# A chunked recurrence's triangular inverse by blocks of 16, and low-rank products in plain fp32 from the rows themselves

## The chip, the cores and the metric

The kernel runs on one core of a Trainium2 chip. Times are device microseconds (us) of that core for one execution, and a kernel's time is the median of its runs. The engines are PE (TensorE: matrix products), DVE (VectorE), ACT (ScalarE), POOL (GpSimd) and SP (which issues transfers). Each works through a queue of its own in order.

## The reference

One inference step of a two-layer encoder in float32, for 1024 new tokens of one stream and 64 of another, with 1024 features. The first layer mixes time with RWKV-7, the second is sliding-window attention; both end in a SwiGLU network. The change lies in the time mixing. `x` is the normalised input, `x_prev` the same rows one token earlier:

```python
xx = x_prev - x
xr, xw, xk, xv, xa, xg = (x + xx * mu[i] for i in range(6))
r, k, v = xr @ w_rkv[0], xk @ w_rkv[1], xv @ w_rkv[2]
w_log = -softplus(-(w0 + tanh(xw @ w1) @ w2)) - 0.5
decay = exp(-exp(w_log))
a = sigmoid(a0 + (xa @ a1) @ a2)
g = sigmoid(xg @ g1) @ g2
...
def step(s, inp):                       # per head, s is 64 x 64
    r_t, w_t, k_t, v_t, a_t, b_t = inp
    sa = einsum('bhvk,bhk->bhv', s, a_t)
    s = s * w_t[:, :, None, :] + sa[..., None] * b_t[:, :, None, :] + v_t[..., None] * k_t[:, :, None, :]
    return s, einsum('bhvk,bhk->bhv', s, r_t)
```

`w1` and `a1` have 64 columns, `g1` has 160 (in the kernel 128, `g1a`, and 32, `g1b`). There are 16 heads of 64.

## The kernel before

Features lie on the partitions, tokens in the columns. The tokens are two halves: A, the first 512, in one group of columns; B, the other 512 and the second stream's 64 (580 columns with those between the streams, in two groups of 290; 576 in two of 288 later). A dense product cuts both operands into two parts of the type float32r, high and low, and adds three products (lines 422 to 424: high by high, low by high, high by low). The parts are made by a copy on ACT and a subtraction on DVE or POOL. The weights stream in from memory and are cut in the same way (lines 382, 383).

The time mixing goes in stages. For each of the six mixed inputs and each of 8 tiles of features, `mix` (from line 663) multiplies the rows on ACT (line 666), adds the preceding rows on DVE (line 667), and cuts the result (lines 414, 415). The mixes for `v`, `r` and `k` feed dense products (`rkv`). Those for `w`, `a` and `g` feed the low-rank products: `low_step` (line 474) adds what a tile of features gives, 2 products for w1, 2 for a1, 3 for g1a and 2 for g1b for each group of columns, and `streamed` hands it the tiles one by one. `decay`, `rate` and `gate` then make the decays, `a` and `g` from the sums. The weights of the low-rank products are cut in `low` (lines 456, 457).

The recurrence takes 64 tokens at a time: 17 chunks, 8 of half A, 8 of half B, and the second stream. For each chunk `prep` makes the triangles of products of keys and queries; `prep2` calls `inverse`; `chain` carries the state through products with the inverse W (line 277 copies what goes into the product with W); `post` normalises the outputs. What doesn't need the state is made a chunk ahead. `inverse` takes (I - T D)^-1 for a strict triangle T of 64 for each of 16 heads. The two diagonal blocks of 32 are solved by substitution on DVE: each partition is a lane that holds a head's block and a fourth of its rows. There are 15 steps of two columns. In each, the rows are in two halves, a multiplication for each half (line 216) and then a reduction for each (line 220), so that no instruction reads what the one right before it has written. Then the block beside the two is made with two rounds of 16 small products (32 by 32) on PE, a copy by ACT and DVE behind each (lines 243 to 255). W is one buffer.

What stands where in the engines' queues is set by a scheduler, from priorities that the code gives: the recurrence stands ahead, and the dense products beside it fill PE's queue. During chunks 0 to 7 those are half B's products for v, r and k, during chunks 8 to 16 the output product of half A's mixing and half A's first SwiGLU network. The queues are fixed when the program is built.

Of the kernel before, what the change touches and what calls it, by code (L numbers as in the profile page):

```python
# [48 lines left out]
class Rwkv:  # L49
    """The chunked WKV-7 recurrence: chunks of 64 tokens, 16 heads in 8 pairs."""  # L50
# [31 lines left out]
    def start(self):  # L82
        """the part of W that stays zero"""
        nc = self.nc
        self.W = self.sb.tile([128, 8, 64], F32, name="W", tag="W", bufs=1)
        nc.gpsimd.memset(self.W, 0.0)

    def prep(self, ch):
        """all that does not need the state; heads 2j on partitions 0-63, heads 2j + 1 on 64-127"""
# [13 lines left out]
        # 1 / |kk|^2 as the lanes of inverse() hold it: [(parity, half of the tokens, 4 times, pair), token]  # L103
# [9 lines left out]
        nl = self.t([128, 32], "nl", 3)  # L113
        V.transpose(out=nl, in_=n4)

        # the products of the decays up to each token, and before it
# [17 lines left out]
        # kk a / P and -kk Pex without the norm of kk, whose square inverse() divides by  # L134
# [3 lines left out]
        # r k r_k  # L138
# [3 lines left out]
        # the four triangles of each head: [(b, k) of the key, (a, r) of the query]  # L142
# [10 lines left out]
        # sum(r k r_k) v  # L153
# [7 lines left out]
    def prep2(self, d):  # L161
# [4 lines left out]
        # the strict triangle of b is spent: a takes its place  # L166
# [13 lines left out]
    def inverse(self, X, nl):  # L180
        """D (I - T D)^-1 of the strict triangles T, transposed, with D = 1 / |kk|^2: first the blocks of 32 by
        substitution, a lane for each block and each fourth of its rows, then the block beside them"""
# [4 lines left out]
        st = self.t([128, 1024], "f4", 2)  # L187
        for q in range(4):
            d = 32 * (q % 2)
            src = Xh[d:d + 32, :, q // 2, d:d + 32].rearrange("p j t -> p t j").unsqueeze(2).broadcast_to([32, 32, 4, 8])  # L190
            S.copy(st[32 * q:32 * q + 32].rearrange("p (t g j) -> p t g j", g=4, j=8), src)  # L191
        N12 = self.t([128, 8, 32], "in12")
        S.copy(N12[0:32], Xh[0:32, :, 0, 32:64])
        S.copy(N12[64:96], Xh[0:32, :, 1, 32:64])
        NL = self.t([128, 1024], "f4", 2)
        V.transpose(out=NL, in_=st)
        NL = NL.rearrange("p (a b) -> p a b", a=32)
        V.tensor_tensor(out=NL, in0=NL, in1=mid(nl, 32), op=ALU.mult)
        # two columns j, j + 1 at a time: row j + 1 takes what it adds by way of column j
        one = NL.rearrange("p a b -> p (a b)")[:, 32:1024:66]  # L200
        ev = NL.rearrange("p (a two) b -> p a two b", two=2)
        # Z: rows 8 r + 4 h + (0 .. 3) in the half h, so that neither half waits for what it has just written
        Z = self.t([128, 1024], "f4", 2).rearrange("p (h c r b) -> p h c r b", h=2, c=4, r=4)
        tm = Z.rearrange("p h c r b -> p (h c r b)")[:, 0:512].rearrange("p (a b) -> p a b", b=32)
        V.tensor_tensor(out=tm, in0=bc(one, 32), in1=ev[:, :, 0, :], op=ALU.mult)
        V.tensor_tensor(out=ev[:, :, 1, :], in0=ev[:, :, 1, :], in1=tm, op=ALU.add)
        for i in (0, 3):
            V.tensor_tensor(out=Z[:, :, i], in0=c["xl0"].rearrange("p (h a b) -> p h a b", h=2, a=4),
                            in1=nl.unsqueeze(1).unsqueeze(1).broadcast_to([128, 2, 4, 32]), op=ALU.mult)
        for j in range(30, 0, -2):  # L210
            # from the first place to the last, and back
            a, b = (0, 3) if j % 4 else (3, 0)
            part = [(h, (j // 4 + 1 - h) // 2) for h in range(2) if (j // 4 + 1 - h) // 2 < 4]
            for h, r0 in part:
                n = 4 - r0
                V.tensor_tensor(out=Z[:, h, 1:3, r0:4, 0:j],  # L216
                                in0=Z[:, h, a, r0:4, j:j + 2].rearrange("p r c -> p c r").unsqueeze(3).broadcast_to([128, 2, n, j]),
                                in1=NL[:, j:j + 2, 0:j].unsqueeze(2).broadcast_to([128, 2, n, j]), op=ALU.mult)
            for h, r0 in part:
                V.tensor_reduce(out=Z[:, h, b, r0:4, 0:j], in_=Z[:, h, min(a, 1):min(a, 1) + 3, r0:4, 0:j].rearrange("p c r j -> p r j c"),  # L220
                                axis=AX.X, op=ALU.add)
        XL = Z[:, :, 0]
        q4 = lambda x: x.rearrange("p h r (q f) -> p h (r q) f", f=4)[:, :, :, 0:2]
        V.tensor_copy(q4(XL), q4(Z[:, :, 3]))
        xe = XL.rearrange("p h r (a two) -> p h r a two", two=2)
        tm = Z[:, :, 1, :, 0:16]
        V.tensor_tensor(out=tm, in0=xe[:, :, :, :, 1], in1=one.unsqueeze(1).unsqueeze(1).broadcast_to([128, 2, 4, 16]), op=ALU.mult)
        V.tensor_tensor(out=xe[:, :, :, :, 0], in0=xe[:, :, :, :, 0], in1=tm, op=ALU.add)
        D3 = self.t([128, 3, 8, 32], "ixd")
        XD, WD, QT = D3[:, 0], D3[:, 1], D3[:, 2]  # L230
        for h in range(2):
            XO = Z[:, h, 1].rearrange("p a b -> p (a b)")                   # [s, (r g pair)]
            V.transpose(out=XO, in_=XL[:, h].rearrange("p a b -> p (a b)"))
        for h in range(2):
            XO = Z[:, h, 1].rearrange("p a b -> p (a b)").rearrange("p (r g j) -> p j r g", r=4, g=4)
            V.tensor_copy(WD.rearrange("p j (r h g) -> p h j r g", r=4, h=2)[:, h], XO)
        V.transpose(out=XD.rearrange("p a b -> p (a b)"), in_=WD.rearrange("p a b -> p (a b)"))
        for q in range(4):
            f = (q % 2) * 32
            e = V.tensor_copy if q % 2 else S.copy  # L240
            e(W[32 * q:32 * q + 32, :, f:f + 32], WD[32 * q:32 * q + 32])
        ps = self.pc()[:, 0:256].rearrange("p (a b) -> p a b", a=8)
        for j in range(8):
            for lo in (0, 64):
                self.mm(ps[lo + 32:lo + 64, j, :], lhsT=N12[lo:lo + 32, j, :], rhs=XD[lo:lo + 32, j, :],
                                 start=True, stop=True)
# [93 lines left out]
class Dense:  # L340
# [124 lines left out]
    def low_step(self, ps, w, k, x, groups):  # L465
# [4 lines left out]
        if k == 7:  # L470
            parts.reverse()
# [90 lines left out]
def tile_stream_step(ctx: ExitStack, tc: tile.TileContext, I, O):  # L562
# [168 lines left out]
    def rate(half, hs, two):  # L731
# [6 lines left out]
        for (o, n), p in zip(groups, ps):  # L738
            dn.stack(y, dn.low_sum(p, 64, n), slice(o, o + n))
# [673 lines left out]
```

## Time and profile before

| | us |
|---|---|
| median of three runs | 3092.23 |
| lowest and highest run | 3085.42, 3095.97 |
| span of the profiled execution | 3098.9 |
| PE busy | 2948.1 |
| DVE busy | 1905.6 |
| ACT busy | 1371.1 |
| POOL busy | 921.6 |
| first PE product of the time mixing starts at | 25.8 |

The profile is one execution; only its span, from the first to the last instruction, is known, and it is longer than the three timed runs. Busy time of PE counts products with modelled ends, so a busy PE may still be slow: the granted clock says how fast it was. Rows of a group read: line, engine, operation, tile written and tiles read, shapes, count, then busy time in us and the mean of one in ns, then the engine's idle time before them and what ended it. Rows of a timeline read: start, length in us, engine, line, operation, tiles, shapes, count.

### The profile page before, as it was taken

How to read it: one execution, taken by the hardware profiler on the slowest of the kernel's cores; microseconds unless marked ns; L12 is line 12 of the kernel's file. 1: busy time of each engine (PE TensorE's matmuls, PEld its weight loads, DVE VectorE, ACT ScalarE, POOL GpSimd, SP SyncE). 2: the span in 40 equal slices, each digit the busy share in tenths (PEclk: the TensorE clock that was granted, in tenths of full speed). 3: DMA queues.
4: the chain of work that ended last, by engine and by line, in shares of the span. 5: the costliest groups of instructions: out<-in, count | busy, mean ns of one | idle time of the engine just before them, and what ended most of it. 6: DMA issues, size and time to landing. Idle time of an engine off the chain costs nothing. (4 is left out here: it accounts for less than half of the span.)

```text
span 3098.9 us, 52449 instructions
## 1 busy us (share of the span) xinstructions
PE 2948.1 (95%) x20126; PEld 2520.6 (81%) x20126; DVE 1905.6 (61%) x3964; ACT 1371.1 (44%) x2489; POOL 921.6 (30%) x768
## 2 busy tenths in 40 slices
PE   6899898998899999999999999999999999999998
PEld 5677677886677777887778999888667889899998
DVE  8887788968898984356654333565555334633334
ACT  6767655434555442344553222344454233322222
POOL 6464233423333322224311222243111222322221
PEclk9998778988899999999999999999999999999999
DMA  4645443334223224332212222222122332322222
GB/s 143 171 121 152 116 123 91 106 99 143 79 83 96 86 66 127 103 112 84 70 45 69 82 82 82 76 84 82 55 65 65 96 96 75 102 83 83 85 85 69
DMA packets 262051, 289.16 MB, mean 93 GB/s; under 512 B 125028, under 2 KB 143972, under 8 KB 261800
## 3 DMA queue, kind: packets, MB, share of 16 engines
q1 hardware_dynamic: 261800, 285.81, 30.8%
q8 instruction: 158, 2.59, 0.3%
q14 instruction: 93, 0.76, 0.1%
HBM read 243.18 MB, written 41.16 MB: 92 GB/s over the span
## 5 line engine op out<-in xcount | busy, mean ns | idle before, releaser
L422 PE MATMUL dp<-xh,wh 128*128 128x288 f32 (+2 forms) x3480 | 1184.5, 342 | 26.5 <-DVE hx L951 7.0
L423 PE MATMUL dp<-xl,wh 128*128 128x288 f32 (+2 forms) x3480 | 1174.9, 338 | 9.5 <-DVE xl L415 6.9
L424 PE MATMUL dp<-xh,wl 128*128 128x288 f32 (+2 forms) x3480 | 1172.3, 337 | 0.0
L382 ACT CAST wh<-wr 128x512 fp32r<-128x512 f32 x730 | 445.8, 619 | 821.7 <-PE dp L423 635.2
L422 PEld LDWEIGHTS dp<-xh,wh 128*128 128x128 f32 x3480 | 669.2, 193 | 100.5 <-DVE hx L951 9.9
L423 PEld LDWEIGHTS dp<-xl,wh 128*128 128x128 f32 x3480 | 669.9, 193 | 72.3 <-DVE xl L415 8.8
L424 PEld LDWEIGHTS dp<-xh,wl 128*128 128x128 f32 x3480 | 670.2, 193 | 61.4 <-issue 5.6
L383 DVE TENSOR_TENSOR wl<-wr,wh 128x512 fp32r<-128x512 f32 x487 | 377.6, 779 | 444.2 <-ACT wh L382 435.5
L383 POOL TENSOR_TENSOR wl<-wr,wh 128x512 fp32r<-128x512 f32 x243 | 336.0, 1383 | 997.3 <-ACT wh L382 894.1
L422 PE MATMUL dp<-mh,wh 128*128 128x288 f32 (+1 forms) x808 | 255.0, 316 | 3.6 <-DVE hx L951 2.6
L424 PE MATMUL dp<-mh,wl 128*128 128x288 f32 (+1 forms) x808 | 254.6, 315 | 0.0
L423 PE MATMUL dp<-ml,wh 128*128 128x288 f32 (+1 forms) x808 | 253.8, 314 | 0.0
L951 DVE TENSOR_TENSOR a_xB<-dp,a_xB 128x288 f32<-128x288 f32 x352 | 158.1, 456 | 82.4 <-PE dp L424 81.9
L932 DVE TENSOR_TENSOR st<-st,dp 128x288 f32<-128x288 f32 (+1 forms) x132 | 70.0, 531 | 216.8 <-PE dp L424 216.4
L934 POOL TENSOR_TENSOR xl<-st,xh 128x288 fp32r<-128x288 f32 (+1 forms) x102 | 101.2, 993 | 334.2 <-ACT xh L933 322.1
L422 PEld LDWEIGHTS dp<-mh,wh 128*128 128x128 f32 x808 | 152.5, 189 | 13.5 <-DVE hx L951 3.8
L424 PEld LDWEIGHTS dp<-mh,wl 128*128 128x128 f32 x808 | 152.4, 189 | 8.1 <-issue 1.8
L423 PEld LDWEIGHTS dp<-ml,wh 128*128 128x128 f32 x808 | 152.6, 189 | 6.8 <-issue 0.8
L951 DVE TENSOR_TENSOR hx<-dp,hx 128x512 f32<-128x512 f32 x176 | 119.8, 685 | 48.2 <-PE dp L424 47.9
L191 ACT COPY r_f<-r_G 32x1024 f32<-32x1024 f32 x68 | 134.7, 1981 | 32.5 <-DVE r_G L152 21.2
L216 DVE TENSOR_TENSOR r_f<-r_f,r_f 128x60 f32<-128x60 f32 (+5 forms) x476 | 117.5, 278 | 0.5
L930 ACT ACTIVATE st<-dp 128x288 f32<-128x288 f32 (+1 forms) x132 | 62.2, 471 | 93.2 <-PE dp L424 92.8
(344 smaller groups left out, 4003.3 us busy)
## 6 DMA issues: line engine op xcount, KB each, us to landing
wr<-in_ffn_in SPq DMA_DIRECT2D x352, 256.0 KB
wr<-in_ffn_out SPq DMA_DIRECT2D x176, 256.0 KB
wr<-in_rkv SPq DMA_DIRECT2D x90, 256.0 KB
wr<-in_rwo SPq DMA_DIRECT2D x32, 256.0 KB
wr<-in_wq SPq DMA_DIRECT2D x32, 256.0 KB
wr<-in_wo SPq DMA_DIRECT2D x32, 256.0 KB
r_r_s<-s_s SPq DMA_DIRECT2D x17, 256.0 KB
r_sv<-s_vt SPq DMA_DIRECT2D x17, 256.0 KB
```

The lines of the kernel that those rows point to most:

```text
L191: S.copy(st[32 * q:32 * q + 32].rearrange("p (t g j) -> p t g j", g=4, j=8), src)
L216: V.tensor_tensor(out=Z[:, h, 1:3, r0:4, 0:j], in0=Z[:, h, a, r0:4, j:j + 2].rearrange("p r c -> p c r").unsqueeze(3).broadcast_to([128, 2 ...
L382: nc.scalar.copy(h, x)
L383: (nc.gpsimd if self.turn % 3 == 0 else nc.vector).tensor_tensor(out=l, in0=x, in1=h, op=ALU.subtract)
L422: self.nc.tensor.matmul(ps, lhsT=wh, rhs=xh, start=i == 0, stop=False)
L423: self.nc.tensor.matmul(ps, lhsT=wh, rhs=xl, start=False, stop=False)
L424: self.nc.tensor.matmul(ps, lhsT=wl, rhs=xh, start=False, stop=i == last)
L930: S.activation(t[o], p, AF.Silu)
L932: V.tensor_tensor(out=t[o], in0=t[o], in1=p, op=ALU.mult)
L934: G.tensor_tensor(out=a.lo[:, q], in0=t[o], in1=a.hi[:, q], op=ALU.subtract)
L951: V.tensor_tensor(out=self.x[m][:, q], in0=p, in1=self.x[m][:, q], op=ALU.add)
```

## The change

Two edits, and nothing else but comments.

The low-rank products take the normalised rows themselves (`h`, with the preceding row in column 0) as plain fp32 operands. The factors of the mix go into the weights: for each tile of features there are two weights, one times 1 - mu for the rows and one times mu for the preceding rows, and the two products add up in one bank. w1 and a1 share a product of 128 columns; g1a and g1b have one each. So the mixes for `w`, `a` and `g` go, with their cuts. Half A's low products stand with the mixes for `v`, half B's in the stage of half A's product for `k`.

The inverse substitutes in blocks of 16: 7 steps, one multiplication and one reduction each, on lanes that hold a block of 16 and half of its rows. Two merges follow, from 16 to 32 and from 32 to 64. The first has two rounds of 32 small products (32 rows, 32 columns, 16 moving columns), with a copy on ACT after the first and an addition and a transposition on DVE after the second. The second is like the one before. A constant that the substitution started from is no longer loaded but made once from the identity matrix.

```diff
     def low_step(self, ps, w, k, h, groups):
         M = w.shape[3]
-        wk = w[:, k].rearrange("p s m -> p (s m)")
-        parts = [(0, 2 * M, x.hi), (0, M, x.lo)] if M <= 64 else [(0, M, x.hi), (M, 2 * M, x.hi), (0, M, x.lo)]
...
         for (o, n), p in zip(groups, ps):
-            for i, (a, b, y) in enumerate(parts):
-                self.nc.tensor.matmul(p[:b - a, :n], lhsT=wk[:, a:b], rhs=y[:, o:o + n],
-                                      start=k == 0 and i == 0, stop=k == 7 and i == len(parts) - 1)
+            for i in range(2):
+                self.nc.tensor.matmul(p[:M, :n], lhsT=w[:, k, i, :], rhs=h[:, o + 1 - i:o + 1 - i + n],
+                                      start=k == 0 and i == 0, stop=k == 7 and i == 1)
...
+    def low(self, parts, tag):
+        nc, n = self.nc, sum(p[1] for p in parts)
+        w, o = self.t([128, 8, 2, n], tag, 1, sb=self.esb), 0
+        for src, M, mu, mu1 in parts:
+            for k in range(0, 8, 4):
+                x = self.raw()[:, :4 * M]
+                nc.sync.dma_start(x, src[:, k * M:k * M + 4 * M])
+                for i, f in enumerate((mu1, mu)):
+                    nc.vector.tensor_tensor(out=w[:, k:k + 4, i, o:o + M], in0=x.rearrange("p (k m) -> p k m", m=M), in1=bc(f[:, k:k + 4], M), op=ALU.mult)
+            o += M
+        return w
...
+    def lora(half, hs, banks):
+        T, groups = mixed[half]
+        n = len(groups)
+        banks["wa"], banks["ga"] = dn.low_banks("rp", n), dn.low_banks("rc", n)
+        if half == "A":
+            banks["gb"] = dn.low_banks("rp", n)
+        for k, h in enumerate(hs):
+            for name in banks:
+                dn.low_step(banks[name], low[name], k, h, groups)
+            yield
...
-    go(first, mixes("A", hA, "v"))
+    go(first, mixes("A", hA, "v"), lora("A", hA, banks["A"]))
...
     def inverse(self, X, nl):
-        for j in range(30, 0, -2):
+        for j in range(14, 0, -2):
             a, b = (0, 3) if j % 4 else (3, 0)
-            part = [(h, (j // 4 + 1 - h) // 2) for h in range(2) if (j // 4 + 1 - h) // 2 < 4]
-            for h, r0 in part:
-                n = 4 - r0
-                V.tensor_tensor(out=Z[:, h, 1:3, r0:4, 0:j],
...
-            for h, r0 in part:
-                V.tensor_reduce(out=Z[:, h, b, r0:4, 0:j], in_=Z[:, h, min(a, 1):min(a, 1) + 3, r0:4, 0:j].rearrange("p c r j -> p r j c"),
-                                axis=AX.X, op=ALU.add)
+            r0, n = j // 2, 8 - j // 2
+            V.tensor_tensor(out=Z[:, 1:3, r0:8, 0:j],
+                            in0=Z[:, a, r0:8, j:j + 2].rearrange("p r c -> p c r").unsqueeze(3).broadcast_to([128, 2, n, j]),
+                            in1=N0[:, j:j + 2, 0:j].unsqueeze(2).broadcast_to([128, 2, n, j]), op=ALU.mult)
+            V.tensor_reduce(out=Z[:, b, r0:8, 0:j], in_=Z[:, min(a, 1):min(a, 1) + 3, r0:8, 0:j].rearrange("p c r j -> p r j c"),
+                            axis=AX.X, op=ALU.add)
...
+        for j in range(8):
+            for q in range(4):
+                o = slice(32 * q, 32 * q + 32)
+                self.mm(ps[o, j, :], lhsT=T(q, j, slice(o.start % 64, o.start % 64 + 32)), rhs=XD[o, j, 0:16], start=True, stop=True)
+        S.copy(Q1[:, :, 0:16], ps)
+        ps = self.pc()[:, 0:128].rearrange("p (a b) -> p a b", a=8)
+        for j in range(8):
+            for q in range(4):
+                o = slice(32 * q, 32 * q + 32)
+                self.mm(ps[o, j, :], lhsT=Q1[o, j, :], rhs=WD[o, j, 16:32], start=True, stop=True)
+        V.tensor_tensor(out=WD[:, :, 16:32], in0=ps, in1=WD[:, :, 16:32], op=ALU.add)
+        turn()
```

More of the change, by code (lines that the diff above doesn't have):

```diff
@@ L194, in inverse @@
[L194 to L204, printed above, removed]
@@ L230, in inverse @@
[L230 to L237, printed above, removed]
@@ L460, in low_banks @@
-    def low_banks(self, tag, groups):
-        self.n += len(groups)
-        return [self.ps.tile([128, 512], F32, name=f"lp_{self.n}_{i}", tag=tag, bufs=2) for i in range(len(groups))]
-    def low_step(self, ps, w, k, x, groups):
+    def low(self, parts, tag):
[8 more added lines that the diff above has]
+            o += M
+        return w
@@ L467, in low_step, with low_banks @@
+    def low_banks(self, tag, n):
+        self.n += n
+        return [self.ps.tile([128, 512], F32, name=f"lp_{self.n}_{i}", tag=tag, bufs=2) for i in range(n)]
+    def low_step(self, ps, w, k, h, groups):
         M = w.shape[3]
[L468 to L471 removed]
         for (o, n), p in zip(groups, ps):
[L473 to L475 removed]
@@ L729, in decay, with rate @@
         summed(*old)
-    def rate(half, hs, two):
+    def rate(half, two, banks):
         T, groups = mixed[half]
-        ps = dn.low_banks("rc", groups)
-        yield from streamed(hs, half, "a", lambda k, x: dn.low_step(ps, low["a1"], k, x, groups))
         two.append(dn.pair(late=half == "B"))
         y = two[0].hi
-        for (o, n), p in zip(groups, ps):
-            dn.stack(y, dn.low_sum(p, 64, n), slice(o, o + n))
+        for (o, n), p in zip(groups, banks["wa"]):
+            q = slice(o, o + n)
+            S.copy(y[64:128, q], p[64:128, :n])
+            V.tensor_tensor(out=y[:64, q], in0=p[64:128, :n], in1=y[64:128, q], op=ALU.subtract)
         yield
@@ L755, in rate, with gate @@
             yield
-    def gate(half, hs, two):
+    def gate(half, hs, two, banks):
         T, groups = mixed[half]
-        pa, pb = (dn.low_banks(t, groups) for t in ("rp", "rc"))
-        def step(k, x):
-            dn.low_step(pa, low["g1a"], k, x, groups)
-            dn.low_step(pb, low["g1b"], k, x, groups)
-        yield from streamed(hs, half, "g", step)
+        yield from lora_late(half, hs, banks)
         sga, gb = dn.t([128, 584], "lo", 2), two[0].lo
-        for (o, n), a, b in zip(groups, pa, pb):
+        for (o, n), a, b in zip(groups, banks["ga"], banks["gb"]):
             S.activation(sga[:, o:o + n], a[:, :n], AF.Sigmoid)
-            x = dn.low_sum(b, 32, n)
-            S.activation(x, x, AF.Sigmoid)
+            x = dn.tmp()[:32, :n]
+            S.activation(x, b[:32, :n], AF.Sigmoid)
             dn.stack(gb, x, slice(o, o + n))
```

153 lines of the change are left out of this document (89 added, 64 removed).

## The prediction

> **What bounds the kernel now.** I read the page's head first (busy time, and the span in 40 slices), then busy time by stage, then the groups of instructions, then the timeline at a few places.
>
> ```profile
> span 3098.9 us, 52449 instructions
> PE 2948.1 (95%) x20126; PEld 2520.6 (81%) x20126; DVE 1905.6 (61%) x3964; ACT 1371.1 (44%) x2489; POOL 921.6 (30%) x768
> DVE  8887788968898984356654333565555334633334
> PEclk9998778988899999999999999999999999999999
> ```
>
> PE is busy nearly throughout, so any product that is added costs time unless PE was waiting or throttled there. Both are found only in the first 15 slices, where DVE stands at 8 and 9 and the granted clock sags. The change touches just that part. So I cut it into stages: the start, the products of half A, the first chunk's preparation, chunks 0 to 7, the gap, chunks 8 to 16. The cuts at 342, 671, 785 and 1181 are the copies of line 277 (once a chunk) of the chunks 0, 7, 8 and 16, so the fifth and the seventh stage hold 7 and 8 whole periods. The first of the 17 is at 342.5, the last at 1181.3:
>
> ```profile
> L277 ACT COPY r_yc<-p_rc x17: 575/586/587, 342.5 to 1181.3; 128x512 f32<-128x512 f32 x17
> ```
>
> ```profile
> core 0: us, PE busy (x) PEld busy (x) DVE busy (x) ACT busy (x) POOL busy (x), PEclk, DMA share, GB/s
> 0.00:26.00 26.00, 4.11 (x11) 2.48 (x12) 19.76 (x24) 14.28 (x25) 15.45 (x26) 1.00 0.67 230
> 26.00:52.00 26.00, 22.96 (x90) 17.14 (x91) 22.77 (x28) 21.05 (x37) 17.44 (x15) 1.00 0.19 56
> 52.00:285.00 233.00, 218.01 (x1121) 178.10 (x1120) 192.62 (x246) 166.84 (x294) 126.05 (x115) 0.96 0.55 153
> 342.00:671.00 329.00, 309.36 (x3141) 267.36 (x3141) 272.98 (x758) 179.52 (x289) 109.05 (x77) 0.84 0.39 107
> 671.00:785.00 114.00, 91.96 (x627) 72.52 (x619) 82.73 (x168) 49.87 (x71) 38.24 (x29) 0.83 0.44 126
> 785.00:1181.00 396.00, 382.98 (x3354) 294.66 (x3352) 353.26 (x932) 196.73 (x271) 136.54 (x102) 0.92 0.27 83
> ```
>
> From 26 to 285 PE is the bound: idle 3.0 + 15.0 = 18 us, clock near 1. In the recurrences a period is 329 / 7 = 47.0 us for the first, 396 / 8 = 49.5 for the second. DVE is busy 39.0 (83%) and 44.2 (89%) of it; the rest of DVE's time goes in waits of its queue for chunk products. PE looks busy too, but at clocks of 0.84 and 0.92 and with fillers: dense products that have to be done anyway. I read these stages as bound by DVE's queue, with PE close behind.
>
> **Prices on PE.** Two dense products that follow each other show what one really takes (start to start; the duration shown holds the pipeline's fill). The first pair of rows has 22 starts of 512 columns between them, the second 46 of 290; the last row is one plain fp32 product, which PE runs as two instructions:
>
> ```profile
> 51.87 0.40 PE L423 MATMUL dp<-el,wh 128*128 128x512 f32 x1
> ...
> 56.95 0.39 PE L424 MATMUL dp<-eh,wl 128*128 128x512 f32 x1
> ```
>
> ```profile
> 317.19 0.30 PE L423 MATMUL dp<-xl,wh 128*128 128x290 f32 x1
> ...
> 323.36 0.30 PE L424 MATMUL dp<-xh,wl 128*128 128x290 f32 x1
> ```
>
> ```profile
> 1371.60 1.02 PE L538 MATMUL dp<-lo,ones 128*128 128x512 f32 x2
> ```
>
> A split product of 512 columns costs 5.08 / 22 = 0.231 us, of 290 columns 6.17 / 46 = 0.134. The plain fp32 product of 512 takes 1.02 less a fill of 0.17 (0.40 - 0.23): 0.85, or 3.7 times as much; of 290 columns, in proportion, 0.48.
>
> **The low-rank products.** Half A has 9 split products for each of 8 tiles of features (2 for w1, 2 for a1, 3 and 2 for the parts of g1): 72 x 0.231 = 16.6 us go. There come 3 groups x 2 rows x 8 tiles = 48 plain ones: 48 x 0.85 = 40.8. Half B: 144 x 0.134 = 19.3 go, 96 x 0.48 = 46.1 come. PE gets 24.2 + 26.8 = **51.0 us** more. On PE the low products lay one by one between the products of v; before (`lp` a low bank, `dp` a dense one, `eh` and `el` a mixed operand's parts):
>
> ```order
> L443 MATMUL dp_292<-el_286,wh_141 128x512
> L443 MATMUL dp_293<-el_286,wh_153 128x512
> L443 MATMUL dp_294<-el_286,wh_165 128x512
> L474 MATMUL lp_0_371<-eh_408,w_35_171 128x512
> L474 MATMUL lp_0_379<-eh_417,a_37_176 128x512
> L474 MATMUL lp_0_371<-el_409,w_35_171 64x512
> ```
>
> and now, as the third to ninth product of the program (`hx` the normalised rows, `x2` the rows and those before them):
>
> ```order
> L508 MATMUL lp_0_230<-hx_72,w_wa_171 128x512 x2
> L508 MATMUL lp_0_231<-hx_72,w_ga_188 128x512 x2
> L508 MATMUL lp_0_232<-hx_72,w_gb_197 32x512 x2
> L478 MATMUL dp_354<-eh_226,wh_135 128x512
> L479 MATMUL dp_354<-eh_226,wl_136 128x512
> ```
>
> All of half A's low products now stand ahead of all but 6 of the 72 first products of v. What they can hide in is the wait for the mixes. What goes off the other engines is 24 mixes a half: of these rows, 48 of the 80 of line 667 and 666 each, and their casts and subtractions.
>
> ```profile
> L667 DVE SCALAR_TENSOR_TENSOR es<-hx,vecs,es 128x512 f32<-128x512 f32 (+1 forms) x80 | 79.1, 1025 | 4.2 <-ACT es L666 3.9 <-POOL hlast L652 0.3
> L666 ACT ACTIVATE es<-hx,mu 128x512 f32<-128x512 f32 (+1 forms) x80 | 56.8, 742 | 17.0 <-POOL el L415 9.5 <-DVE el L415 3.4 <-DVE hx L645 2.4
> ```
>
> That is 49 us of DVE and 36 of ACT in this stage, but those engines weren't the bound. The most it can return is PE's 18 us idle and the 4% of clock in 218 us, 9 us: 27 together. I take 20, and set the longer preparation of the weights on DVE (16 multiplications for 5 subtractions, ahead of the first product) inside it. So this part costs **+31 us**; bounds +24 (all 27 returned) and +51 (nothing).
>
> **The inverse, on DVE.** Blocks of 16 instead of 32: 7 steps of one multiplication and one reduction instead of 15 steps in two halves, 14 instructions a chunk instead of 56. Before, in DVE's queue:
>
> ```order
> L216 TENSOR_TENSOR r_f_67_2967<-r_f_67_2967,r_f_66_2964 128x2x24
> L216 TENSOR_TENSOR r_f_67_2967<-r_f_67_2967,r_f_66_2964 128x2x20
> L220 TENSOR_REDUCE r_f_67_2967<-r_f_67_2967 128x24
> L220 TENSOR_REDUCE r_f_67_2967<-r_f_67_2967 128x20
> L216 TENSOR_TENSOR r_f_67_2967<-r_f_67_2967,r_f_66_2964 128x2x2x22
> ```
>
> and now:
>
> ```order
> L234 TENSOR_TENSOR r_f_117_2969<-r_f_117_2969,r_f_116_2965 128x2x2x12
> L237 TENSOR_REDUCE r_f_117_2969<-r_f_117_2969 128x2x12
> L234 TENSOR_TENSOR r_f_117_2969<-r_f_117_2969,r_f_116_2965 128x2x3x10
> L237 TENSOR_REDUCE r_f_117_2969<-r_f_117_2969 128x3x10
> L318 COPY r_sv_2829<-p_rc_2869 64x8x64
> ```
>
> Fewer, but none has another one between itself and what it reads. Prices:
>
> ```profile
> 444.17 0.32 DVE L216 TENSOR_TENSOR r_f<-r_f,r_f 128x56 f32<-128x56 f32 x2
> 444.41 0.38 DVE L220 TENSOR_REDUCE r_f<-r_f 128x28 f32<-128x84 f32 x2
> 444.71 0.32 DVE L216 TENSOR_TENSOR r_f<-r_f,r_f 128x52 f32<-128x52 f32 x2
> ```
>
> ```profile
> L216 DVE TENSOR_TENSOR r_f<-r_f,r_f 128x60 f32<-128x60 f32 (+5 forms) x476 | 117.5, 278 | 0.5
> L220 DVE TENSOR_REDUCE r_f<-r_f 128x30 f32<-128x90 f32 (+5 forms) x476 | 97.9, 237 | 0.8
> L208 DVE TENSOR_TENSOR r_f<-c_xl,r_nl 128x256 f32<-128x256 f32 x34 | 26.1, 808 | 0.3
> L198 DVE TENSOR_TENSOR r_f<-r_f,r_nl 128x1024 f32<-128x1024 f32 x17 | 25.0, 1470 | 0.2
> L196 DVE STREAM_TRANSPOSE r_f<-r_f 128x1024 f32<-128x1024 f32 x17 | 21.1, 1243 | 34.8 <-ACT r_f L191 34.8
> L206 DVE TENSOR_TENSOR r_f<-r_f,r_f 128x512 f32<-128x512 f32 x17 | 16.2, 954 | 0.3
> L205 DVE TENSOR_TENSOR r_f<-r_f 128x512 f32<-128x512 f32 x17 | 15.6, 916 | 0.2
> ```
>
> Four of the small ones take 444.71 - 444.17 = 0.54 us undisturbed, so 56 take between 7.6 and (117.5 + 97.9) / 17 = 12.7; I take 10. The 14 new ones run one after another, at the 0.24 that the two groups' means give less a little for size: 3.3. The five larger groups are 104.0 / 17 = 6.1 a chunk on two to four times the elements; I take 2.9 after. The rest stays, and the second merge adds some seven instructions of 0.1 to 0.4: +1.1. DVE saves 6.7 + 3.2 - 1.1 = **8.8 us a chunk** (6 to 11).
>
> **What a shorter chunk is worth.** A period that shrinks gives its fillers back to be done later. Counted in the program, the dense products between the chunks' products with W fall from 964 (of 290) to 506 in the first recurrence and from 912 (of 512) to 578 in the second: 458 x 0.134 = 61.4 and 334 x 0.231 = 77.2 us move behind the recurrences, 138.6 together. With them some 3 and 4 us a period of DVE's work on fillers moves. DVE's busy time becomes 39.0 - 8.8 - 3 = 27 and 44.2 - 8.8 - 4 = 31 us. If it stays the bound at its shares of 83% and 89%, the periods are 33 and 35; if the shares fall to 75% and 80%, as other waits come to the fore, 36 and 39. I take about the middle, 35.0 and 37.5: 7 x 12.0 + 8 x 12.0 = 180 us, less 138.6: **-41**. The first inverse of each recurrence lies open, PE idle 114.0 - 92.0 = 22 us in the gap at 671 alone: **-8**.
>
> The new merge adds 64 small products a chunk, 128 instructions on PE. The nearest row:
>
> ```profile
> L73 PE MATMUL p_rc<-r_ixd,r_in 32*32 32x32 f32 x544 | 14.1, 202 | 6.5 <-DVE r_ixd L237 6.5
> ```
>
> At 14.1 / 544 = 26 ns that is 3.3 us a chunk, 57 in all; it lies inside the periods, covered as long as DVE ends them, and is PE's time lost if not. The Trainium skill (TensorE: Matmul & The Clock Gate, Part 3) says that products in different 32-row and 32-column strips of the array start about 4 ns apart; by that, since the new ones use four strips where the row's use two, the 57 would be an estimated 9. No row here uses four.
>
> **The sum**: 3098.9 + 31 - 41 - 8 = 3081. The profiled span lies 6.7 us above the median of the runs, 3092.2 (what lies around the span isn't shown), so **3074 us**, 0.6% faster. 0.3%, 9 us, is about what a measurement of this kernel can tell.
>
> **Rivals.** *DVE stays the bound.* Periods of 33 and 35 give 7 x 14 + 8 x 14.5 = 214, less 138.6 = -75; with +31 and -8 that is 3047 on the span, 3040 as a median. For it: DVE's 8s and 9s in the slices.
>
> *Slower: the trips between PE, ACT and DVE end the period.* The merge of the second chunk shows what such trips cost:
>
> ```profile
> 381.96 0.36 ACT L247 COPY r_ixd<-p_rc 32x256 f32<-32x256 f32 x1
> ...
> 391.94 0.36 ACT L254 COPY W<-p_rc 32x256 f32<-32x256 f32 x1
> ```
>
> Two copies of 0.36 us, 10 us apart, each behind what stood ahead in in-order queues. The change adds two such trips. If periods fall only to 40 and 43, the gain is 7 x 7 + 8 x 6.5 = 101, 38 less than the fillers moved: 3098.9 + 31 + 38 - 8 = 3160, 3153 as a median. The point of decision: the periods must shrink by (138.6 + 31 - 8) / 15 = 10.8 us, to 36.2 and 38.7; above that, the change loses. For it: fewer fillers leave PE emptier, and the clock is already lower (0.84) where a period holds less dense work. The Trainium skill (same page, Part 1) says that the clock halves after an idle window of some 3.4 us; by that rule the stretch slows further; the rows here show only the means.
>
> *No difference*: periods near 36.5 and 39. *The edits not doing what they say*: the order shows them done; nothing given.
>
> **Chances.** Forecast (3045 to 3083) 0.33, DVE the bound 0.17, no difference 0.17, slower 0.33. Faster 0.50, same 0.17, slower 0.33. The range runs from 3010 (DVE the bound and its saving near 11) to 3135 (most of the slower case); the likeliest case alone is 3045 to 3083.
>
> **What would show it.** Line 508 taking 80 to 90 us of PE, its first block before the products of v; the inverse's small steps (lines 234, 237) at 3 to 4 us a chunk; the copies of the line after U0 35 to 38 us apart; clock in the recurrences no lower than 0.8. Wrong would be: periods over 39, the first chunk's preparation starting much later than 285 + 31 = 316, or PE idle behind the new merge's copies.

## The result, and the profile after

The changed kernel takes 3182.14 us (median of four runs, 3178.52 to 3186.44), the kernel before 3090.47 in the runs beside it (3085.42 to 3095.97). The ratio is 1.0294, with a 95% interval of 1.0275 to 1.0314: 2.9% slower. The page of the profile after:

```profile
span 3176.7 us, 56106 instructions
...
PE 3039.1 (96%) x22374; PEld 2572.6 (81%) x22374; DVE 1714.1 (54%) x3262; ACT 1243.5 (39%) x2364; POOL 843.4 (27%) x739
...
DVE  4634777844888754336754333475555343633334
...
PEclk9999878799888889999999999999999999999999
```

DVE lost 191 us of work, ACT 128, and PE gained 91: the time went PE's way (+78 on the span). Stage by stage, cut at the same events as before (the copies of what goes into the product with W, now line 314, for the chunks 0, 7, 8 and 16):

```profile
28.00:76.00 48.00, 48.00 (x108) 16.95 (x108) 14.86 (x20) 14.72 (x23) 9.14 (x11) 1.00 0.03 11
76.00:316.00 240.00, 228.24 (x1010) 176.39 (x1009) 112.10 (x163) 101.11 (x181) 64.69 (x79) 0.96 0.49 133
316.00:389.00 73.00, 62.80 (x573) 54.24 (x573) 54.73 (x118) 39.46 (x67) 20.96 (x21) 0.81 0.45 135
389.00:669.00 280.00, 260.03 (x3589) 217.05 (x3586) 209.15 (x453) 142.25 (x254) 85.84 (x66) 0.79 0.37 100
669.00:833.00 164.00, 151.56 (x1250) 133.13 (x1245) 91.68 (x162) 66.79 (x117) 52.44 (x41) 0.95 0.51 141
833.00:1184.00 351.00, 334.75 (x4059) 260.98 (x4058) 265.38 (x570) 146.37 (x226) 114.21 (x89) 0.84 0.25 74
```

The first row is half A's low products, one solid block at full clock. Periods fell from 47.0 to 280 / 7 = 40.0 us and from 49.5 to 351 / 8 = 43.9, DVE's share of them to 75% and 76% (from 83% and 89%). But the granted clock fell from 0.84 to 0.79 and from 0.92 to 0.84. The shortened recurrences pay back 49 + 45 = 94 us; the gap (114 to 164) and all behind chunk 16 (1918 to 1993) are 125 us longer, and hold 460 and 338 dense products more, counted in the traces (458 and 334 were forecast to move); and the first chunk's copy comes 47 us later.

### The profile page after: what moved, and what is told of

Read it like the earlier page. It is cut to its first block, busy times and chain, and to the rows that moved or that the text cites. A ratio compares the mean times of both kernels' runs of the same rounds, so it can differ in the third digit from the quotient of the medians.

```text
span 3176.7 us, 56106 instructions
## 1 busy us (share of the span) xinstructions
PE 3039.1 (96%) x22374; PEld 2572.6 (81%) x22374; DVE 1714.1 (54%) x3262; ACT 1243.5 (39%) x2364; POOL 843.4 (27%) x739
## 5 line engine op out<-in xcount | busy, mean ns | idle before, releaser
L420 DVE TENSOR_TENSOR wl<-wr,wh 128x512 fp32r<-128x512 f32 x487 | 369.7, 762 | 534.2 <-ACT wh L419 523.7
L420 POOL TENSOR_TENSOR wl<-wr,wh 128x512 fp32r<-128x512 f32 x243 | 329.5, 1356 | 1140.8 <-ACT wh L419 1043.2
L73 PE MATMUL p_rp<-r_AR,r_BK 64*128 64x128 f32 x544 | 95.7, 349 | 19.6 <-DVE r_G L170 9.4
L73 PEld LDWEIGHTS p_rp<-r_AR,r_BK 64*128 64x128 f32 x544 | 81.8, 244 | 27.7 <-DVE r_G L170 10.7
L969 ACT CAST xh<-st 128x288 fp32r<-128x288 f32 (+1 forms) x102 | 50.2, 492 | 123.8 <-DVE st L968 122.6
```

The source lines that it names most:

```text
L73: self.nc.tensor.matmul(*a, **k)
L420: (nc.gpsimd if self.turn % 3 == 0 else nc.vector).tensor_tensor(out=l, in0=x, in1=h, op=ALU.subtract)
L969: S.copy(a.hi[:, q], t[o])
```

## The experiments

To sort the runs I split each span in two. **Work**: every product counted at one price for its form, the mean of the fastest 60% of its steps from end to end, over the traces of all runs; that is PE's time at full clock. **Lost**: the rest of the span, in which PE waited or ran at half clock. **Half clock** is worked out from the mean granted clock c: its records know full and half only, so it is 2 x (1 - c) x span. These three are of the profiled execution, in us; that of the kernel before is 4 to 9 us longer than the medians in the table, so a difference of spans from it comes out smaller than one of medians. What each label stands for is said with the runs below; before_nosub, no_merge, no_merge_act, merge_few and merge_prod leave out or replace a part of the inverse, so they count for their time alone.

| run | time, us | ratio to before | work | lost | half clock |
|---|---|---|---|---|---|
| before | 3090 to 3095 | 1 | 2604 | 495 | 297 |
| changed | 3182 | 1.0294 | 2673 | 504 | 330 |
| low_only | 3153 | 1.0201 (1.0184 to 1.0218) | 2657 | 495 | 284 |
| inv_only | 3129 | 1.0121 (1.0105 to 1.0138) | 2620 | 506 | 338 |
| low_late | 3168 | 1.0246 (1.0222 to 1.0269) | 2673 | 487 | 297 |
| after_post | 3195 | 1.0333 (1.0314 to 1.0352) | 2673 | 521 | 377 |
| before_nosub | 3088 | 0.9987 (0.9972 to 1.0003) | 2604 | 485 | 309 |
| after_dve | 3189 | 1.0304 (1.0277 to 1.0331) | 2673 | 521 | 345 |
| no_merge | 3108 | 1.0046 (1.0029 to 1.0063) | 2661 | 442 | 242 |
| merge_few | 3121 | 1.0101 (1.0085 to 1.0116) | 2669 | 450 | 243 |
| merge_prod | 3175 | 1.0281 (1.0263 to 1.0298) | 2673 | 495 | 329 |
| after_fill | 3198 | 1.0336 (1.0303 to 1.0370) | 2738 | 452 | 217 |
| after_bd | 3214 | 1.0392 (1.0359 to 1.0424) | 2720 | 490 | 353 |
| inv_bd | 3161 | 1.0215 (1.0190 to 1.0241) | 2668 | 491 | 341 |
| before_bd | 3122 | 1.0096 (1.0069 to 1.0123) | 2654 | 466 | 281 |
| before_pool | 3074 | 0.9932 (0.9913 to 0.9951) | 2604 | 471 | 252 |
| before_pool4 | 3166 | 1.0249 (1.0227 to 1.0272) | 2604 | 570 | 394 |
| after_pool | 3156 | 1.0214 (1.0190 to 1.0238) | 2673 | 485 | 335 |
| before_split | 3098 | 1.0016 (1.0001 to 1.0032) | 2604 | 494 | 260 |
| no_merge_act | 3107 | 1.0044 (1.0028 to 1.0060) | 2661 | 445 | 242 |

**Each edit alone.** Two kernels, each with one of the two edits whole.

> The low-rank products of the changed kernel, with the inverse of the kernel before (blocks of 32, one merge). Sorts the 92 us lost by the two edits. Theory (the trips through the two merges end the period, and the low products cost what the first chunk's delay shows): the first chunk's U0 comes 47 us later than before, the periods stay at 47.0 and 49.5 us, and the time is about 3090 + 47 = 3137 us; the rest of the loss belongs to the inverse. The prediction on record made it +31, 3121. Rival (PE's throughput): since PE is given 51 us of work and is full, it is +51 or more, 3141 to 3150. Rival (the recurrence hides part of the delay): under 3110.

> The inverse by blocks of 16 of the changed kernel, with the low-rank products of the kernel before. Theory (trips): periods as in the changed kernel, 40 and 44 us, fillers moved behind the recurrences, and the time is 3182 - 47 = 3135 us, 45 slower than before. The prediction's own terms (-41 - 8) gave 3041 here. Rival (the inverse is neutral, and the low products hurt the recurrences as well, by the clock): 3090, with periods shorter than 40 and 44.

59 us for the low products and 35 for the inverse: 94, and both together 92. They add up. The low products are work and nothing else: +53, with the lost time unchanged. The new inverse brings 16 of work and 11 more lost, though DVE has some 8 us a chunk less to do.

**Place and order.** Half A's low products among the products of v, and post's transposes behind the merges' products in PE's queue.

```diff
-    go(first, mixes("A", hA, "v"), lora("A", hA, banks["A"]))
+    go(first, mixes("A", hA, "v"))
...
-    go(rkv("A", "v", xs["Av"], ws), take(2, chain(take(1, de), take(1, ra))), mixes("A", hA, "r", True))
+    go(rkv("A", "v", xs["Av"], ws), chain(lora("A", hA, banks["A"]), take(2, chain(take(1, de), take(1, ra)))), mixes("A", hA, "r", True))
```

> The changed kernel, with half A's 48 low products taken from the head of the program and put among the products of v of half A, the mixes of v starting first as before. Theory (price: the plain fp32 products cost 51 us on an engine that is full, wherever they stand): within 10 us of 3182. Rival (place: at the head they hold back the products of v while DVE, ACT and POOL run ahead and then wait): 15 to 30 us below 3182, and the first chunk's U0 at 365 to 375 in place of 389.

```diff
-            rw.two.at(base + late, low + late)
+            rw.two.at(base + 0.2 + late, low + late)
             rw.post(ch, d, Y)
```

> The changed kernel, with one number of the priorities altered: the transposes of the outputs of a chunk (on PE, behind POOL's scaling) go behind the products of the merges in PE's queue, not between them. In the changed kernel the last 12 of the 32 products of the second merge wait some 5 us behind those transposes. Theory (the chain through the merges ends the period): the periods shrink by 3 to 5 us, and the time falls by 30 to 60 us, to 3120 to 3150. Rival (PE's throughput ends the period, the queue's order only moves idle time about): periods stay within 1 us, time within 10 us of 3182. Rival (clock): periods shrink, but the mean clock falls below 0.79 and 0.84 with them, and the time stays above 3160.

```profile
L314 ACT COPY r_yc<-p_rc x17: 585/585/593, 377.8 to 1158.0; 128x512 f32<-128x512 f32 x17
```

Among the products of v the low products cost 14 us less, between the two expectations, and the first of these copies comes at 378 instead of 389. The work is the same (2673); the lost time falls from 504 to 487. So most of the price stays, but a part of it was the place. The transposes between the merge's products looked like the loss in a timeline, and moving them cost 13 us, with 377 us at half clock for 330: that reading of mine fell.

**What DVE's time is worth.** The 15 steps left out of the kernel before; 26 dummy multiplications put into the changed one.

```diff
-        for j in range(30, 0, -2):
...
-                V.tensor_reduce(out=Z[:, h, b, r0:4, 0:j], in_=Z[:, h, min(a, 1):min(a, 1) + 3, r0:4, 0:j].rearrange("p c r j -> p r j c"),
-                                axis=AX.X, op=ALU.add)
```

> The kernel before, without the 15 steps of the substitution (56 small instructions of DVE a chunk, 7.6 to 12.7 us of its queue; the output is then not the reference's). Nothing else goes and no trip is added, so it asks what DVE's time in the inverse is worth by itself. Measured so far: with the new inverse alone, PE's time at full clock rose by 17 us and what PE lost to waits and half clock stayed (495 us before, 505 with it). Theory 1 (what PE loses in a chunk doesn't hang on DVE's time, since the order written for PE takes the fillers out of a shorter chunk): 3092 within 15, although the periods fall to about 36 to 42 us. Theory 2 (DVE's time is worth something, 3 us a chunk for 8.8 as the prediction had it, and in the changed kernel the new trips took it back): about 3020.

```diff
+        for _ in range(26):
+            V.tensor_scalar(out=Z[:, 0], in0=Z[:, 0], scalar1=1.0, scalar2=None, op0=ALU.mult)
         XL = Z[:, 0]
```

> The changed kernel with 26 multiplications by 1.0 in place (128x128, in SBUF) behind the 7 steps of the substitution, 0.3 us each: about 8 us a chunk are given back to DVE, what the change had saved. Theory 1: the periods rise by about 8 us with fillers put into them, and the time stays within 15 of 3182. Theory 2 (DVE's time counts): 30 to 50 us above 3182.

Next to nothing, both ways: DVE's busy time fell by 159 us in the one (1905.6 to 1746.7) and rose by 100 in the other (1714.1 to 1814.3), and the kernels' times moved by 5 and 6. The two recurrences of the kernel without the steps, and then of the one with the dummies:

```profile
326.60:588.40 261.80, 243.81 (x2657) 204.99 (x2657) 190.36 (x347) 163.22 (x254) 92.75 (x65) 0.79 0.36 101
762.10:1096.60 334.50, 307.13 (x2994) 240.14 (x2994) 259.24 (x449) 176.64 (x237) 124.45 (x92) 0.86 0.26 81
```

```profile
399.40:737.60 338.20, 324.89 (x4021) 280.67 (x4022) 260.71 (x650) 156.70 (x283) 101.52 (x78) 0.83 0.36 103
848.70:1257.20 408.50, 388.59 (x4299) 300.52 (x4300) 331.77 (x786) 160.35 (x251) 127.46 (x99) 0.88 0.24 77
```

Without the steps the periods are 37.4 and 41.8 us (47.0 and 49.5 in its parent), with the dummies 48.3 and 51.1 (40.0 and 43.9). So the periods went with DVE's time, and yet each kernel stays within 7 us of its parent. A longer chunk takes more fillers, a shorter one fewer, and the clock goes with them (0.79 and 0.86 for 0.84 and 0.92; 0.83 and 0.88 for 0.79 and 0.84). What PE loses in the whole run moves by 10 and 17 us.

**What the first merge is made of.** Without it (lines 263 to 275 left out); with its two trips but one wide product for each 32 small ones; with its 64 small products but no trips.

> The changed kernel without the first merge: its 64 small products a chunk, the copy on ACT, the addition and the second transposition are left out (the output is then not the reference's). Theory 1 (as for the kernel without the substitution): only the products go, 17 us at full clock, so 3160 to 3168. Theory 2 (the two new trips take back what DVE saved, some 3 us a chunk): 17 + 50 us, about 3115.

```diff
-        for j in range(8):
-            for q in range(4):
-                o = slice(32 * q, 32 * q + 32)
-                self.mm(ps[o, j, :], lhsT=T(q, j, slice(o.start % 64, o.start % 64 + 32)), rhs=XD[o, j, 0:16], start=True, stop=True)
+        self.mm(ps, lhsT=X[:, 0, :], rhs=XD[:, :, 0:16], start=True, stop=True)
```

> The changed kernel with one product of 128x128 by 128 columns in place of each group of 32 small ones in the first merge (2 products a chunk for 64; the output is then not the reference's). The copy on ACT, the addition and the transposition on DVE, and so both trips, stay. Without the whole merge the kernel took 3108. If the 64 products are what costs (issue and throughput of PE): 3110 to 3125. If the two trips cost, whatever runs in them: 12 to 20 us below 3182 for the products' own time at full clock, 3160 to 3172.

```diff
-        S.copy(Q1[:, :, 0:16], ps)
...
-        V.tensor_tensor(out=WD[:, :, 16:32], in0=ps, in1=WD[:, :, 16:32], op=ALU.add)
-        turn()
```

> The changed kernel with the 64 small products of the first merge, but without its trips: the copy on ACT, the addition and the second transposition on DVE are left out, and nothing reads what the products give (the output is not the reference's). So far: neither products nor trips 3108, trips with 2 products 3121, trips with 64 products 3182. If the 64 products cost by themselves, in PE's queue (61 us of the 74): 3155 to 3170. If they cost only together with the trips, because PE waits at each with fewer fillers behind it: 12 us for their time at full clock, 3115 to 3130.

Neither 3108, trips 3121, products 3175, both 3182. **The products cost 61 to 67 us, the trips 7 to 13.** Until then I had held the trips for the culprit; this took it back. A second group of 32, in the changed kernel's timeline of PE:

```profile
485.95 0.29 PE L459 MATMUL dp<-xh,wh 128*128 128x290 f32 x1
486.18 0.73 PE L73 MATMUL p_rc<-r_ixd,Q 32*32 32x16 f32 x64
486.83 0.37 PE L73 MATMUL p_rp<-r_AR,r_BK 64*128 64x128 f32 x1
```

From 486.18 to the next start, 0.65 us for 32 products: 1.3 a chunk, some 22 in all (12 at the prices of the table, which leave out waits and the clock). The rest shows in the clock, of the kernel without the merge (first two rows) and of the one with the products alone, in the two recurrences:

```profile
376.90:643.30 266.40, 251.49 (x2722) 215.00 (x2722) 200.34 (x460) 142.78 (x250) 86.66 (x66) 0.83 0.40 111
796.40:1122.40 326.00, 311.86 (x3046) 242.09 (x3044) 272.97 (x581) 149.81 (x226) 121.91 (x94) 0.91 0.27 87
```

```profile
383.20:665.20 282.00, 265.93 (x3596) 226.66 (x3596) 197.24 (x445) 141.44 (x246) 87.64 (x65) 0.78 0.35 98
831.10:1181.40 350.30, 329.77 (x4030) 260.46 (x4032) 262.40 (x561) 142.45 (x217) 118.52 (x93) 0.84 0.25 78
```

Over the whole run the small products raise the time at half clock from 242 to 329 us, and half of that difference, some 44, is lost where PE has work to do: 22 + 44 = 66 us, against the 65 by which the spans differ (3102.8 and 3167.4). The recurrences hold 541 and 619 dense products without the merge and 513 and 572 with the small products, counted in the traces; that is too near for the fillers alone to explain the clock, but how much of it is theirs isn't separated.

**Work put into the trips.**

```diff
+        fill = lambda t: [self.mm(t[:, 128:512], lhsT=c["id"], rhs=X.rearrange("p a b -> p (a b)")[:, 384 * i:384 * i + 384], start=True, stop=True) for i in range(3)]
...
+        fill(t)
         S.copy(Q1[:, :, 0:16], ps)
...
+        fill(t)
         V.tensor_tensor(out=WD[:, :, 16:32], in0=ps, in1=WD[:, :, 16:32], op=ALU.add)
```

> The changed kernel with 3 extra plain fp32 products of 384 columns (0.64 us each) on PE behind each of the two groups of products of the first merge, so that they can run while ACT and DVE work on the merge: 102 products, 65 us at full clock, whose results are not used. If PE's waits in the trips of the merges are real and uncovered: most of it lies in the waits and the clock is held up, so under 25 us above 3182. If PE's throughput is the bound there (the queue holds other work to do at that place): 55 to 70 us above 3182.

66 us of useless work cost 15. Both recurrences:

```profile
388.10:683.10 295.00, 283.79 (x3734) 227.12 (x3736) 200.14 (x453) 141.65 (x254) 85.93 (x66) 0.88 0.36 100
839.70:1197.20 357.50, 346.45 (x4140) 258.26 (x4140) 256.06 (x557) 142.58 (x222) 114.63 (x89) 0.92 0.23 72
```

The clock rises from 0.79 and 0.84 to 0.88 and 0.92; time at half clock falls by 113 us, half of which is 56, and the lost time by 52. So PE's emptiness there is real, and it costs by the clock more than by the waits.

**Fewer, larger products.** The blocks of four strips in one weight of 128x128 that is zero elsewhere: 8 products a group for 32. To fill that weight takes four more copies a chunk on POOL, and four copies on ACT and DVE for the one behind the first group.

```diff
+                self.mm(ps[:, j, :], lhsT=Q1[:, j, :], rhs=XD[:, j, 0:16], start=True, stop=True)
...
+            self.mm(ps[:, j, :], lhsT=Q1[:, j, :], rhs=WD[:, j, 16:32], start=True, stop=True)
```

> The changed kernel with the first merge by 16 products a chunk instead of 64: the blocks of four strips stand in one weight of 128x128 that is zero elsewhere (8 products a group). Both trips stay; the output is the reference's. With 2 products a chunk the kernel took 3121, with 64 it took 3182, although the 64 take only 1.3 us a chunk at full clock in the trace. In the order written for PE, dense products between the chunks' products with W were 506 and 579 with 64 small products, 674 and 710 with 2, and are 667 and 653 here. If the number of small products costs because fillers stand in the order in proportion to it: 3120 to 3140. If it was the left-out work itself (its data, its readers): 3170 to 3185.

> A version meant to be better than both: the low products of the kernel before, the inverse by blocks of 16, the first merge by 16 products of block weights, and two of the four copies ahead of the substitution on POOL. By the runs: 3129 for the new inverse alone, less 45 to 55 for the fewer small products, less 20 for the copies: 3055 to 3070. If the effects don't add up, as both fill the same waits: 3080 to 3090.

> The kernel before with two of the four copies on POOL (3074), and its merge by 16 products of block weights for 32 small ones; two small buffers lose a copy to make room. The order holds 949 and 850 dense products in the recurrences, where the kernel with the copies on POOL alone has 1004 and 842, so no more fillers. If fillers are what counts: 3065 to 3080. If the number of small products counts by itself, as 61 us for 62 a chunk would say: 16 us less, under 3060.

All three missed. The products of the first merge in the changed kernel with block weights:

```profile
L73 PE MATMUL p_rc<-r_ixd,Q 128*128 128x16 f32 x544 | 74.7, 279 | 6.8 <-DVE r_ixd L258 5.3 <-DVE Q L271 1.5
L73 PEld LDWEIGHTS p_rc<-r_ixd,Q 128*128 128x128 f32 x544 | 72.5, 213 | 11.9 <-issue 4.1 <-DVE Q L271 1.8 <-DVE r_ixd L258 1.7
```

An instruction takes 74.7 / 544 = 137 ns, eight products 2.2 us, where 32 small ones take 0.65. The loads of the weights go in step, 72.5 / 544 = 133 ns each: a full weight for 16 columns. Against the changed kernel lost time fell by 14 and work rose by 47; inv_bd against inv_only gives 15 and 48, with two copies on POOL besides, and before_bd against before_pool 50 of work. The order holds 161 and 74 more fillers in the two recurrences than the changed kernel's, merge_few's 168 and 131; so the count of fillers doesn't settle the time either.

**ACT and POOL.** Of the four copies ahead of the substitution, two on DVE, two on POOL or all on POOL; two on POOL in the changed kernel; each issued twice in the kernel without the merge.

```diff
-            S.copy(st[32 * q:32 * q + 32].rearrange("p (t g j) -> p t g j", g=4, j=8), src)
+            (G.tensor_copy if q % 2 else S.copy)(st[32 * q:32 * q + 32].rearrange("p (t g j) -> p t g j", g=4, j=8), src)
```

> The kernel before, with two of the four copies that feed the substitution moved from ACT to DVE: ACT loses some 4 us a chunk, DVE gains about as much. Theory A: 20 to 40 us below 3093, since DVE's time has been shown to be worth nothing. Theory B: within 12 of 3093.

> The kernel before, with the same two copies moved from ACT to POOL, which is busy only 30% of the span. Theory A: 20 to 40 us below 3093, if POOL is no slower at such a copy than some 4 us; later if it is, as the inverse then starts later. Theory B: within 12 of 3093, or slower by what POOL holds back.

> The kernel before, with all four of those copies on POOL. If ACT's time is worth something: 10 to 20 us below 3074. If the two halves running beside each other on ACT and POOL are what gave the 20 us: back to 3085 to 3095, as four in a row on one engine are no shorter than before.

> The changed kernel, with two of the four copies that feed the substitution moved from ACT to POOL, as in the kernel before, where that gave 20 us (11.6 of them in what PE lost in the front and the gap, where the first inverse lies open). If the gain comes from a shorter start of each inverse: 10 to 20 us below 3182, since the copies are half as long here. If it was a matter of the order only: within 10.

> The kernel without the first merge (its output is not the reference's), with each of the four copies that feed the substitution (ACT, 1.1 us each) issued twice: 4.4 us of ACT a chunk come back, most of the 5 to 6 us that the change had taken from ACT. It asks why the kernel without the first merge is 45 us faster than the one with the old inverse and the same low products, when taking 12 us a chunk from DVE alone had given 5. Theory A (ACT's queue is worth something, since each trip and the copy of U0 pass through it): 35 to 50 us above 3108, 3143 to 3158. Theory B (ACT's time is worth as little as DVE's; the difference lies in something else, as the smaller operations on DVE or the copies of W): within 12 of 3108.

Two copies on POOL give 20 us in the kernel before and 26 in the changed one, more than either expectation. The kernel before with two on POOL, **3074 us, 0.7% under the kernel before**, is the fastest of all that leave nothing out. All four on POOL cost 2.5%, where 3085 to 3095 was the most expected. ACT's time by itself is worth nothing in the kernel without the merge (no_merge_act). The copies of the kernel with two on POOL:

```profile
L191 POOL COPY r_f<-r_G 32x1024 f32<-32x1024 f32 x34 | 69.0, 2029 | 58.5 <-DVE r_G L152 39.4 <-DVE r_f L227 17.5 <-DVE r_f L228 0.9
L191 ACT COPY r_f<-r_G 32x1024 f32<-32x1024 f32 x34 | 67.1, 1973 | 50.5 <-DVE r_G L152 34.0 <-DVE r_f L227 16.3
```

A copy takes as long on either engine, so two halves beside each other take 4 us instead of 8. But a shorter start of the inverse doesn't explain the other two runs: four in a row on POOL should have taken the time of the kernel before and came 76 us above it, with periods of 58 us; and the copies split with DVE (before_split) should have gained as well, and gained nothing. The cause of the 20 us stays open.

## Why the prediction was wrong

**The low products** were priced right and credited wrongly. The rows of line 508 after, and of line 474 before, over the whole span:

```profile
0.00:3177.00 3177.00, 93.93 (x288) 46.23 (x288) 0.95 0.31 91
```

```profile
0.00:3099.00 3099.00, 44.41 (x216) 30.92 (x216) 0.95 0.31 93
```

+49.5 of PE, where the prediction had 51.0. The step that failed is "I take 20" of the 27 us that might come back. Nothing came: the first instruction of the first chunk's preparation (POOL, line 101 before, 117 after) moved from 265.5 to 316.0, 50.5 us for the 31 forecast.

```profile
L101 POOL TENSOR_TENSOR r_rt<-r_r_k,vecs x17: 1040/1351/2244, 265.5 to 1038.7; 128x512 f32<-128x512 f32 x17
```

```profile
L117 POOL TENSOR_TENSOR r_rt<-r_r_k,vecs x17: 1037/1088/1548, 316.0 to 1054.4; 128x512 f32<-128x512 f32 x17
```

The 285 of the prediction's sign is the first copy ahead of the substitution (284.4), which came at 334.2 (line 211 after), 18 past the 316. What went off DVE and ACT didn't shorten what PE lost there: the lost time of the front stayed at 60 us (63 in low_only). The block of low products at the head runs while DVE is busy 14.9 us of 48 (the first row after); among the products of v, low_late had 14 us back.

**The inverse on DVE.** Its rows stand for 4.3 us a chunk (72.8 / 17, some 3.3 forecast), and the time in which DVE works on the inverse fell from 21.8 to 13.5 us a chunk, added up from the traces (lines 196 to 255 before, 216 to 292 after), 8.4 for a forecast 8.8:

```profile
L234 DVE TENSOR_TENSOR r_f<-r_f,r_f 128x28 f32<-128x28 f32 (+3 forms) x119 | 44.8, 377 | 2.8
L237 DVE TENSOR_REDUCE r_f<-r_f 128x14 f32<-128x42 f32 (+3 forms) x119 | 28.0, 235 | 3.0
```

"I read these stages as bound by DVE's queue" was right of the periods, which went with DVE's time in before_nosub and after_dve, and failed as a price: the recurrences of before_nosub are 67 and 62 us shorter than before, and the whole kernel 5. So the step that failed here is "180 us, less 138.6": what the periods gave came back as fillers and half clock, and -41 was not to be had from DVE's time. A busy share of 89% said nothing of what that time was worth. That the order fixed at building keeps it so, by giving each chunk the fillers that its length has room for, is argued; no run held the fillers still.

**The small products** are the step that turned the sign: they lie "inside the periods, covered as long as DVE ends them". The 57 us by the row of 26 ns were close to what they cost (61 to 67), but they stood in the sum at nothing. Their own time was smaller, 22 us. By the Trainium skill (TensorE: Matmul & The Clock Gate, Part 3), with starts 4 ns apart, it would have been an estimated 9; the 64 instructions above take 0.65 us, 10 ns each, and that decides. The other 44 us go with the time at half clock.

**The sum by its terms.** Low products +31 forecast, +53 on the span (3151.6 - 3098.9). The inverse without its first merge: -41 - 8 forecast, -49 measured (3102.8 - 3151.6). The agreement is partly luck: by the lost time, 31 of it lie in the front and the gap, where the first inverses lie open, and 23 in the periods (4 of work go against them); what in the rest of the inverse gave those wasn't found. The first merge: 0 forecast, +74 (3176.7 - 3102.8).

**The rival that was slower** gave periods of 40 and 43 and 3153 us; they came out at 40.0 and 43.9, above its break-even of 36.2 and 38.7. Its sign was right. Its periods were right by luck: the trips that it named cost 13 us alone, and with the products but no trips the periods are 40.3 and 43.8 already (282.0 / 7 and 350.3 / 8). Of the 29 us by which it was short, 22 are the low products. Its sentence on the clock held: time at half clock went from 297 to 330 us.

## What to carry to other kernels

Where fillers make up each period, don't price a shorter chain by its period: split the span into PE's work at full clock and what PE loses, and ask which of the two an edit changes. Work added to a full PE cost its whole price here in the place first chosen for it, however idle the engines beside it became, and a quarter less in another. Small products cost some three times their own time here: price them by leaving them out, and look at the granted clock of the stage before and after. Fewer products with full weights in their place cost more still.

## What the runs showed of the hardware

**What keeps the clock up.** In all traces, stretches of half clock last multiples of 3.41 us (but the last one, which the end cuts off). I cut the stretch from 30 to 1250 us of 20 traces into 7,125 windows of that length and counted in each the columns that PE streamed (twice for an instruction of plain fp32), each product by its share of the 128 rows in use. A window filled with dense products reaches some 7,600. Of 828 windows under 2,000, 827 were followed by half clock; of 537 from 2,000 to 2,800, 507; of 310 up to 3,200, 148; of 599 up to 4,000, 56; of 4,851 above, 21. The limit is near 3,000 both at full and at half clock. By columns without the rows 665 windows fall on the wrong side of the best limits, by rows 216, by rows and columns of the array 337. The counts move by some tens with how a product across a border is divided. By this fit a 32-row product counts for a quarter of its time, which goes with the cost of the small products; it is a fit to records, and no run changed the rows alone. The Trainium skill (TensorE: Matmul & The Clock Gate, Part 1) has the clock halve after an idle window; here windows that were two fifths full were enough.

**Other numbers.** A plain fp32 product with a full weight and 16 columns takes 2 x 137 ns, four strips of 32 rows side by side 2 x 10 ns each. A strided copy of 32x1024 takes 1.97 us on ACT, 2.03 on POOL, and 1.20 on DVE:

```profile
L191 DVE COPY r_f<-r_G 32x1024 f32<-32x1024 f32 x34 | 40.7, 1197 | 1.0
```
